# Where operands start in the partition: weight tiles, activations and gap tiles at chosen bytes modulo 128

## The chip, the cores and the metric

One core of one Trainium2 chip runs the kernel as a single program. TensorE (PE in the profile) multiplies, VectorE (DVE), ScalarE (ACT) and GpSimd (POOL) do the elementwise work, SyncE (SP) issues most DMAs. The metric is device time in microseconds of one execution; the median of the runs counts.

## What is computed

A decoder trunk of two layers on x of 256 positions and 1,024 features, in float32. Each layer is a mixer between two half-step SwiGLU FFNs; the first mixer is a chunked gating layer, the second stick-breaking attention whose keys and values come from x ahead of the layer. Cut to what matters:

```python
def swiglu(h, w_in, w_out):                     # w_in 1024 x 5632, w_out 2816 x 1024
    gate, up = jnp.split(h @ w_in, 2, axis=-1)
    return (jax.nn.silu(gate) * up) @ w_out

def chunked_sgu(h, w_in, ln_g, ln_b, w_s, b_s, w_out):
    u, v = jnp.split(jax.nn.gelu(h @ w_in), 2, axis=-1)     # 2048 each
    v = layer_norm(v, ln_g, ln_b)
    ...  # v mixed along positions in chunks of 128 by causal w_s, plus b_s
    return (u * v) @ w_out

def reference(x, ...):
    for i in range(2):
        if i == 1:
            k_shared, v_shared = ...            # rms_norm(x, kv_norm) @ w_kv
        x = x + 0.5 * swiglu(rms_norm(x, ffn_norm[i, 0]), ffn_w_in[i, 0], ffn_w_out[i, 0])
        h = rms_norm(x, mix_norm[i])
        if i == 0:
            x = x + chunked_sgu(h, ...)
        else:
            x = x + stick_breaking_attention(h @ b_w_q[0], k_shared, v_shared) @ b_w_o[0]
        x = x + 0.5 * swiglu(rms_norm(x, ffn_norm[i, 1]), ffn_w_in[i, 1], ffn_w_out[i, 1])
    return rms_norm(x, final_norm)
```

## The kernel before

Activations are kept with features on the 128 partitions: `xT` is x, `xnh` and `xnl` are its normalised high and low parts. Every product is made of three float32r matmuls on such parts (`mm3`): high by low, low by high, high by high, at lines 148 to 150. `split` (line 152) makes the parts of an activation: a ScalarE copy rounds to the high part, a VectorE subtraction leaves the low part.

Weights come as units of 128 x 1,024 float32 (512 KB), in the fixed order in which they are used; `W.add` notes the source of each while the stages are planned. `Weights.run_to` issues their loads on SyncE into seven `raw` buffers and splits each into `whi` (ScalarE, line 81) and `wlo` (VectorE, line 83), nine buffers of each; `Weights.get` runs both some units ahead of their use. There are two kinds:
- First matrices (`cols`): 512 rows by 256 columns of a weight that multiplies x. In gate and up (`ga`, `ua` for the first FFN, then b, c, d), u (`uu`), q and k (`kT`) the weight is the stationary operand and x (`xnh`, `xnl`; `xkh`, `xkl` for k) the moving one, 256 columns. In v (`v`) x is stationary and the weight moves.
- Second matrices (`rows`): 128 rows by 1,024 columns of an output weight. In the FFNs a to c and in the gating layer (`ya`, `yb`, `yc`, `ys`) the weight is stationary and the hidden values `hh`, `hl` of pool `hp` move, 256 columns; in attention's output (`yo` from `oTh`, `oTl`) likewise. In the last FFN (`yo` from `hhd`, `hld`) `hh` and `hl` are stationary and the weight moves, 512 columns.

An FFN runs in eleven steps: 96 matmuls of gate and up for 256 hidden features, and 48 of the output projection two steps behind. While TensorE works on one unit, the loads and splits of later ones go on beside it. Each matmul loads its own stationary operand; TensorE takes all in program order.

Where a tile lies in its partition follows from the order in which the pools are opened (lines 125 to 132, then `sgu`, `att` and `fin`, which take turns in the same space), from the sizes of their tiles, rounded up to 32 bytes, and from what stands ahead: 16,384 bytes of scratch for descriptors and four constants of 32 bytes each. Added up, the places modulo 128 are:

| operand | tiles | bytes modulo 128 |
|---|---|---|
| x | `xT`, `xnh`, `xnl` | 32 |
| loaded weights | `raw` | 96 |
| parts of first and second matrices | `whi`, `wlo` | 96 |
| hidden values, q, attention weights | `hh`, `hl`, `qh`, `ql`, `a0`, `a1` in `hp` | 96 |
| keys, values of attention | `kzh`, `kzl`, `vdh`, `vdl` | 0 |
| x for k and v, attention's output | `xkh`, `xkl`, `oTh`, `oTl` | 0 |
| identity, ones | `ident`, `ones` | 96 |

All slices of these that a matmul reads start at multiples of 512 bytes from the tile's start, so they have the same remainder.

Of the kernel before, what the change touches and what calls it, by code (L numbers as in the profile page):

```python
# [8 lines left out]
F32 = mybir.dt.float32  # L9
F32R = mybir.dt.float32r  # L10
# [5 lines left out]
P = 128  # L16
T = 256
# [5 lines left out]
UNIT = 1024  # L23
# [15 lines left out]
class Weights:  # L39
# [3 lines left out]
    def __init__(self, tc, raw_pool, hi_pool, lo_pool):  # L43
        self.nc = tc.nc
        self.keep_order = tc.keep_in_program_order
        self.strict = False
        self.behind = 0
        self.piece = UNIT
        self.pools = raw_pool, hi_pool, lo_pool
        self.sources = []  # L50
        self.raw = {}
        self.parts = {}
        self.loaded = 0
        self.split = 0

    def add(self, source):
        self.sources.append(source)
        return len(self.sources) - 1

    def order(self, ins):  # L60
# [3 lines left out]
    def run_to(self, load, split):  # L64
        nc = self.nc
        while self.loaded < min(load, len(self.sources)):
            i = self.loaded
            raw = self.pools[0].tile([P, UNIT], F32, tag="raw", name=f"raw{i}")
            src = self.sources[i]
            view = raw if len(src.shape) == 2 else raw.rearrange("p (k c) -> p k c", k=src.shape[1])  # L70
            nc.sync.dma_start(view, src)
            self.raw[i] = raw
            self.loaded += 1
        while self.split < min(split, len(self.sources)):
            i = self.split
            raw = self.raw.pop(i)
            hi = self.pools[1].tile([P, UNIT], F32R, tag="whi", name=f"whi{i}")
            lo = self.pools[2].tile([P, UNIT], F32R, tag="wlo", name=f"wlo{i}")
            for c in range(0, UNIT, self.piece):
                cc = slice(c, c + self.piece)  # L80
                ins = nc.scalar.copy(hi[:, cc], raw[:, cc])  # L81
                self.order(ins)
                ins = nc.vector.tensor_sub(lo[:, cc], raw[:, cc], hi[:, cc].bitcast(F32))  # L83
                self.order(ins)
                if self.behind:
                    self.keep_order(ins)
                    self.behind -= 1
            self.parts[i] = hi, lo
            self.split += 1
# [10 lines left out]
def trunk(  # L100
# [20 lines left out]
    nc = tc.nc  # L121
    x = x[0]
    out = out[0]

    const = ctx.enter_context(tc.tile_pool(name="const", bufs=1))
    act = ctx.enter_context(tc.tile_pool(name="act", bufs=1))
    rawp = ctx.enter_context(tc.tile_pool(name="rawp", bufs=7))
    hip = ctx.enter_context(tc.tile_pool(name="hip", bufs=9))
    lop = ctx.enter_context(tc.tile_pool(name="lop", bufs=9))
    hp = ctx.enter_context(tc.tile_pool(name="hp", bufs=4))  # L130
    scr = ctx.enter_context(tc.tile_pool(name="scr", bufs=8))
    small = ctx.enter_context(tc.tile_pool(name="small", bufs=3))
# [12 lines left out]
    def mm3(o, a, b, first, last):  # L145

        (ah, al), (bh, bl) = a, b
        nc.tensor.matmul(o, al, bh, start=first, stop=False, skip_group_check=True)  # L148
        nc.tensor.matmul(o, ah, bl, start=False, stop=False, skip_group_check=True)  # L149
        nc.tensor.matmul(o, ah, bh, start=False, stop=last, skip_group_check=True)  # L150
# [15 lines left out]
    W = Weights(tc, rawp, hip, lop)  # L166

    def cols(w, c0, kh):
        return w[kh * 512 : (kh + 1) * 512, c0 : c0 + 256].rearrange("(k p) c -> p k c", p=P)

    def rows(w, r0):
        return w[r0 : r0 + P, :]

    def plan_in_out(n, ins, w_out):


        steps = {}
        for j in range(n + 1):
            if j < n:
                steps["in", j] = [[W.add(cols(w, c0 + 256 * j, kh)) for w, c0 in ins] for kh in range(2)]  # L180
            if j:
                steps["out", j - 1] = [W.add(rows(w_out, 256 * (j - 1) + P * m)) for m in range(2)]
        return steps

    def plan_ffn(i, s):
        return plan_in_out(NPAIR, [(ffn_w_in[i, s], 0), (ffn_w_in[i, s], DFF)], ffn_w_out[i, s])
# [3 lines left out]
    plan_u = {}  # L190
    for step in U_STEPS:
        kind, j = step
        if kind == "in":
            plan_u[step] = [W.add(cols(a_w_in[0], 256 * j, kh)) for kh in range(2)]
        elif kind == "out":
            plan_u[step] = [W.add(rows(a_w_out[0], 256 * j + P * m)) for m in range(2)]
    plan01 = plan_ffn(0, 1)
    plan_kv = [[W.add(cols(w_kv, 256 * j, kh)) for kh in range(2)] for j in range(2)]
    plan10 = plan_ffn(1, 0)
    plan_q = [[W.add(cols(b_w_q[0], 256 * j, kh)) for kh in range(2)] for j in range(4)]  # L200
    plan_o = [W.add(rows(b_w_o[0], P * b)) for b in range(8)]
    plan11 = plan_ffn(1, 1)


# [59 lines left out]
    acc = act.tile([P, T], F32, name="acc")  # L264
    rT = act.tile([P, 2], F32, name="rT")

    spare = act.tile([P, P + 1 + 2 * (T + 1)], F32, name="spare")
    rb = spare[:, :T]
    diag = spare[:, T : 2 * T].rearrange("p (n t) -> p n t", n=2)

# [18 lines left out]
            nc.scalar.activation(s, xT[:, d, :], AF.Square)  # L289
            nc.gpsimd.tensor_add(acc, acc, s)  # L290

    eps = const.tile([P, 1], F32, name="eps")
    nc.vector.memset(eps, RMS_EPS)

    def newton(o, root, v, w):
# [79 lines left out]
    class Residual:  # L375
# [8 lines left out]
        def add(self, w, h, first, last, ds=range(KC)):  # L384
            for d in ds:
                mm3(
                    self.at(d), tuple(t[:, d * P : (d + 1) * P] for t in w), h, first and d % 2 == 0, last
                )
# [234 lines left out]
    for kind, j in U_STEPS:  # L623
# [4 lines left out]
        else:  # L628
            h = hs.pop(j)
            for m in range(2):  # L630
                w = W.get(plan_u["out", j][m], UNIT)
# [7 lines left out]

    att = ExitStack()  # L640
    at = att.enter_context(tc.tile_pool(name="att", bufs=1))
    kz = [at.tile([P, 4, 2, T], F32R, name=f"kz{p}") for p in "hl"]
    vd = [at.tile([P, 2, 4, 2, 64], F32R, name=f"vd{p}") for p in "hl"]
    xkh = at.tile([P, KC, T], F32R, tag="bigh", name="xkh")
    xkl = at.tile([P, KC, T], F32R, tag="bigl", name="xkl")
    for t in kz:
# [265 lines left out]
```

## Time and profile before

| | before |
|---|---|
| median of 3 runs | 1003.92 us (1003.63 to 1004.09) |
| profiled execution | 1004.4 us |
| its span, first to last instruction | 1002.7 us |
| PE busy | 982.3 us (98%), 8042 matmul records |
| DVE, ACT, POOL busy | 645.2 us, 504.1 us, 86.5 us |
| DMA | 179.56 MB, 179 GB/s on average |

The profile is of one execution. Matmuls are pipelined: one starts long before the one ahead of it has ended, so a recorded duration of 276 ns doesn't mean that the next one starts 276 ns later. How close they follow is read from the start times in the timeline.

### The profile page before, as it was taken

To read this page: it belongs to the slowest core of one execution; us is meant where nothing else is said; L and a number is where in the kernel's file an instruction comes from. 1 tells how busy PE (TensorE), PEld (TensorE's weight loads), DVE (VectorE), ACT (ScalarE), POOL (GpSimd) and SP (SyncE) were. 2 spreads that over 40 slices of the span, in tenths; PEclk is the share of its full clock that TensorE was granted. 3 is DMA by queue.
4 is the path that set the end of the run, shared out by engine and by line. 5 is a ranking of instruction groups with operands and counts; after the bars stand their busy time and mean duration, and the time that the engine had idled before them with its cause. 6 is when DMAs were issued, how large, how long until landed. Compare 5 with 4: busy or idle time off the path is not lost.

```text
span 1002.7 us, 19306 instructions
## 1 busy us (share of the span) xinstructions
PE 982.3 (98%) x8042; PEld 963.5 (96%) x8042; DVE 645.2 (64%) x823; ACT 504.1 (50%) x690; POOL 86.5 (9%) x126
## 2 busy tenths in 40 slices
PE   8999999999999999999999999999997899999996
PEld 8999999999999999999999999999997899999996
DVE  6864675675866775656569755555678775565644
ACT  6643434475544564444448444444487674444433
POOL 4000000020000300000003000000046320000002
PEclk9999999999999999999999999999999999999999
DMA  9966565647555455666564866665643346656511
GB/s 304 322 195 190 169 189 188 190 143 222 184 177 175 133 191 188 193 188 193 186 195 146 247 189 191 189 193 186 190 149 92 97 147 191 207 172 203 176 42 43
DMA packets 135208, 179.56 MB, mean 179 GB/s; under 512 B 5624, under 2 KB 119376, under 8 KB 135120
## 3 DMA queue, kind: packets, MB, share of 16 engines
q1 hardware_dynamic: 134768, 177.76, 56.7%
q8 instruction: 63, 1.03, 0.4%
q0 software_dynamic: 192, 0.52, 0.2%
q14 instruction: 25, 0.20, 0.1%
q10 hardware_dynamic: 160, 0.05, 0.0%
HBM read 176.73 MB, written 1.05 MB: 177 GB/s over the span
## 4 chain that ended last, share of the span: by engine, by line
PE 89%; DVE 5%; ACT 2%; issue 1%; DMA 1%; POOL 1%; SPq 0%; ACTq 0%; POOLq 0%; DVEq 0%
PE yo L148 2%; PE yo L150 2%; PE yo L149 2%; PE yb L148 2%; PE yb L150 2%; PE yb L149 2%; PE ud L148 2%; PE ud L150 2%; PE gd L148 2%; PE ud L149 2%; PE gb L148 2%; PE gd L150 2%; PE gd L149 2%; PE ub L148 2%; PE gc L150 2%; PE gb L150 2%
## 5 line engine op out<-in xcount | busy, mean ns | idle before, releaser
L81 ACT CAST whi<-raw 128x1024 fp32r<-128x1024 f32 (+1 forms) x333 | 342.7, 1045 | 391.0 <-issue 205.3
L83 DVE TENSOR_TENSOR wlo<-raw,whi 128x1024 fp32r<-128x1024 f32 (+1 forms) x333 | 402.1, 1225 | 200.9 <-ACT whi L81 200.0
L290 POOL TENSOR_TENSOR acc<-acc,sq 128x256 f32<-128x256 f32 x39 | 33.8, 867 | 387.5 <-ACT sq L289 385.6
L148 PE MATMUL ga<-xnh,wlo 128*128 128x256 f32 x176 | 50.1, 285 | 0.0
L148 PE MATMUL ya<-hha,wlo 128*128 128x256 f32 x176 | 49.9, 284 | 0.2 <-DVE xT L399 0.2
L148 PE MATMUL yc<-hhc,wlo 128*128 128x256 f32 x176 | 49.9, 284 | 0.1
L148 PE MATMUL yb<-hhb,wlo 128*128 128x256 f32 x176 | 49.9, 284 | 0.0
L149 PE MATMUL ga<-xnl,whi 128*128 128x256 f32 x176 | 49.3, 280 | 0.5 <-DVE xnl L277 0.5
L149 PE MATMUL ya<-hla,whi 128*128 128x256 f32 x176 | 49.7, 282 | 0.0
L148 PE MATMUL gd<-xnh,wlo 128*128 128x256 f32 x176 | 49.7, 282 | 0.0
L149 PE MATMUL yb<-hlb,whi 128*128 128x256 f32 x176 | 49.7, 282 | 0.0
L149 PE MATMUL yc<-hlc,whi 128*128 128x256 f32 x176 | 49.7, 282 | 0.0
L150 PE MATMUL yb<-hhb,whi 128*128 128x256 f32 x176 | 49.6, 283 | 0.0
L148 PE MATMUL ua<-xnh,wlo 128*128 128x256 f32 x176 | 49.1, 279 | 0.5 <-DVE wlo L83 0.5
L150 PE MATMUL ya<-hha,whi 128*128 128x256 f32 x176 | 49.4, 283 | 0.0
L150 PE MATMUL gd<-xnh,whi 128*128 128x256 f32 x176 | 49.4, 281 | 0.0
L150 PE MATMUL ud<-xnh,whi 128*128 128x256 f32 x176 | 49.4, 281 | 0.0
L148 PE MATMUL ud<-xnh,wlo 128*128 128x256 f32 x176 | 49.4, 281 | 0.0
L149 PE MATMUL ud<-xnl,whi 128*128 128x256 f32 x176 | 49.4, 281 | 0.0
L149 PE MATMUL gd<-xnl,whi 128*128 128x256 f32 x176 | 49.4, 281 | 0.0
L150 PE MATMUL yc<-hhc,whi 128*128 128x256 f32 x176 | 49.4, 283 | 0.0
L150 PE MATMUL ga<-xnh,whi 128*128 128x256 f32 x176 | 49.1, 279 | 0.0
(289 smaller groups left out, 3353.6 us busy)
## 6 DMA issues: line engine op xcount, KB each, us to landing
raw<-in_ffn_w_in_dram SPq DMA_DIRECT2D x176, 512.0 KB, 4.5
raw<-in_ffn_w_out_dram SPq DMA_DIRECT2D x88, 512.0 KB, 4.3
raw<-in_a_w_in_dram SPq DMA_DIRECT2D x32, 512.0 KB, 4.4
raw<-in_a_w_out_dram SPq DMA_DIRECT2D x16, 512.0 KB, 3.3
raw<-in_b_w_q_dram SPq DMA_DIRECT2D x8, 512.0 KB, 4.5
raw<-in_b_w_o_dram SPq DMA_DIRECT2D x8, 512.0 KB, 4.0
raw<-in_w_kv_dram SPq DMA_DIRECT2D x4, 512.0 KB, 4.0
xin<-in_x_dram SPq DMA_DIRECT2D x4, 256.0 KB, 4.9
```

What stands on the lines that cost most here:

```text
L81: ins = nc.scalar.copy(hi[:, cc], raw[:, cc])
L83: ins = nc.vector.tensor_sub(lo[:, cc], raw[:, cc], hi[:, cc].bitcast(F32))
L148: nc.tensor.matmul(o, al, bh, start=first, stop=False, skip_group_check=True)
L149: nc.tensor.matmul(o, ah, bl, start=False, stop=False, skip_group_check=True)
L150: nc.tensor.matmul(o, ah, bh, start=False, stop=last, skip_group_check=True)
L290: nc.gpsimd.tensor_add(acc, acc, s)
```

## The change

Only places change; no instruction is added or taken away. `W.add` takes a place, in elements, and the tiles of `whi` and `wlo` become 32 elements wider, of which 1,024 from that place on are used: 0 for first matrices, 16 (64 bytes) for second ones. Gap tiles of 32, 128, 32 and 64 bytes are put between pools or tiles, `eps` is padded to 128 bytes and `spare` to 2,688, and the descriptor scratch shrinks to 8,192 bytes, which makes room. Added up in the same way, x comes to 0 modulo 128, `raw` to 64, the parts of first matrices to 64 and those of second ones to 0, `hp` to 64, the keys and values stay at 0, `xkh`, `xkl`, `oTh` and `oTl` come to 64, `ident` and `ones` stay at 96.

```diff
-    def add(self, source):
+    def add(self, source, place=0):
         self.sources.append(source)
+        self.places.append(place)
         return len(self.sources) - 1
...
-            hi = self.pools[1].tile([P, UNIT], F32R, tag="whi", name=f"whi{i}")
-            lo = self.pools[2].tile([P, UNIT], F32R, tag="wlo", name=f"wlo{i}")
+            hi, lo = (
+                pool.tile([P, UNIT + 32], F32R, tag=f"w{p}", name=f"w{p}{i}")[:, self.places[i] : self.places[i] + UNIT]
+                for pool, p in zip(self.pools[1:], ("hi", "lo"))
+            )
...
+    def gap(name, size):
+        pool = ctx.enter_context(tc.tile_pool(name=name, bufs=1))
+        pool.tile([P, size // 4], F32, name=f"{name}t")
...
+    gap("gapw", 32)
     rawp = ctx.enter_context(tc.tile_pool(name="rawp", bufs=7))
     hip = ctx.enter_context(tc.tile_pool(name="hip", bufs=9))
     lop = ctx.enter_context(tc.tile_pool(name="lop", bufs=9))
+    gap("gaph", 128)
     hp = ctx.enter_context(tc.tile_pool(name="hp", bufs=4))
...
-                steps["out", j - 1] = [W.add(rows(w_out, 256 * (j - 1) + P * m)) for m in range(2)]
+                steps["out", j - 1] = [W.add(rows(w_out, 256 * (j - 1) + P * m), 16) for m in range(2)]
...
-            plan_u[step] = [W.add(rows(a_w_out[0], 256 * j + P * m)) for m in range(2)]
+            plan_u[step] = [W.add(rows(a_w_out[0], 256 * j + P * m), 16) for m in range(2)]
...
-    plan_o = [W.add(rows(b_w_o[0], P * b)) for b in range(8)]
+    plan_o = [W.add(rows(b_w_o[0], P * b), 16) for b in range(8)]
...
-    spare = act.tile([P, P + 1 + 2 * (T + 1)], F32, name="spare")
+    spare = act.tile([P, P + 1 + 2 * (T + 1)], F32, name="spare", padded_shape=[P, 672])
...
-    eps = const.tile([P, 1], F32, name="eps")
+    eps = const.tile([P, 1], F32, name="eps", padded_shape=[P, 32])
...
+    at.tile([P, 8], F32, name="gapk")
     kz = [at.tile([P, 4, 2, T], F32R, name=f"kz{p}") for p in "hl"]
     vd = [at.tile([P, 2, 4, 2, 64], F32R, name=f"vd{p}") for p in "hl"]
+    at.tile([P, 16], F32, name="gapx")
     xkh = at.tile([P, KC, T], F32R, tag="bigh", name="xkh")
...
-    nc = _bacc.Bacc("TRN2", target_bir_lowering=False, num_devices=1)
+    nc = _bacc.Bacc("TRN2", target_bir_lowering=False, num_devices=1, dynamic_dma_scratch_size=8192)
```

## Rows read from the trace of the kernel before

**Rows 1.** The page: span, busy time of TensorE, and its granted clock in 40 slices

```profile
span 1002.7 us, 19306 instructions
PE 982.3 (98%) x8042; PEld 963.5 (96%) x8042; DVE 645.2 (64%) x823; ACT 504.1 (50%) x690; POOL 86.5 (9%) x126
...
PEclk9999999999999999999999999999999999999999
```

**Rows 2.** The page: the chain that ended last, by engine

```profile
PE 89%; DVE 5%; ACT 2%; issue 1%; DMA 1%; POOL 1%; SPq 0%; ACTq 0%; POOLq 0%; DVEq 0%
```

**Rows 3.** Waits of TensorE, the longest: total us, times, longest us

```profile
PE o L149 <- DVE a0l L154: 6.1, 3, 3.5
```

**Rows 4.** Timeline, FFN c gate and up: start us, us, engine, line; 46 starts apart

```profile
590.59 0.28 PE L148 MATMUL gc<-xnh,wlo 128*128 128x256 f32 x1
...
595.80 0.28 PE L149 MATMUL uc<-xnl,whi 128*128 128x256 f32 x1
```

**Rows 5.** Timeline, FFN d gate and up, 46 starts apart

```profile
856.17 0.28 PE L148 MATMUL gd<-xnh,wlo 128*128 128x256 f32 x1
...
861.59 0.28 PE L149 MATMUL ud<-xnl,whi 128*128 128x256 f32 x1
```

**Rows 6.** Timeline, FFN c output projection, 37 starts apart

```profile
567.77 0.28 PE L150 MATMUL yc<-hhc,whi 128*128 128x256 f32 x1
...
572.21 0.28 PE L148 MATMUL yc<-hhc,wlo 128*128 128x256 f32 x1
```

**Rows 7.** Timeline, FFN d output projection, 512 columns, 19 starts apart

```profile
866.97 0.39 PE L149 MATMUL yo<-wlo,hhd 128*128 128x512 f32 x1
...
871.28 0.39 PE L150 MATMUL yo<-whi,hhd 128*128 128x512 f32 x1
```

**Rows 8.** Timeline, attention's output projection, 22 starts apart

```profile
797.07 0.28 PE L149 MATMUL yo<-oTl,whi 128*128 128x256 f32 x1
...
799.66 0.28 PE L150 MATMUL yo<-oTh,whi 128*128 128x256 f32 x1
```

**Rows 9.** Timeline, the transposes of x after FFN d's first steps, merged

```profile
830.78 1.91 PE L819 MATMUL xb<-ident,xT 128*128 128x128 f32 x16
```

**Rows 10.** Groups by line: out<-in, shape, count, busy us, mean ns, idle before

```profile
L149 PE MATMUL yc<-hlc,whi 128*128 128x256 f32 x176 | 49.7, 282 | 0.0
L149 PE MATMUL gd<-xnl,whi 128*128 128x256 f32 x176 | 49.4, 281 | 0.0
L150 PE MATMUL yc<-hhc,whi 128*128 128x256 f32 x176 | 49.4, 283 | 0.0
L149 PE MATMUL ga<-xnl,whi 128*128 128x256 f32 x176 | 49.3, 280 | 0.5 <-DVE xnl L277 0.5
L149 PE MATMUL ua<-xnl,whi 128*128 128x256 f32 x176 | 48.9, 278 | 0.0
L149 PE MATMUL gb<-xnl,whi 128*128 128x256 f32 x176 | 48.8, 277 | 0.0
L149 PE MATMUL gc<-xnl,whi 128*128 128x256 f32 x176 | 48.6, 276 | 0.0
L149 PE MATMUL ys<-hls,whi 128*128 128x256 f32 x128 | 36.2, 283 | 0.0
L149 PE MATMUL v<-wlo,xnh 128*128 128x256 f32 x128 | 35.7, 279 | 0.0
L149 PE MATMUL uu<-xnl,whi 128*128 128x256 f32 x128 | 35.6, 278 | 0.0
L149 PE MATMUL q<-xnl,whi 128*128 128x256 f32 x64 | 17.9, 279 | 0.0
L149 PE MATMUL yo<-oTl,whi 128*128 128x256 f32 x64 | 17.8, 280 | 0.0
```

**Rows 11.** Stretch of 17 us in FFN c: busy us of each engine, clock, DMA share

```profile
567.00:584.00 17.00, 17.00 (x149) 17.00 (x149) 9.93 (x12) 7.52 (x10) 0.00 (x0) 1.00 0.68 202
```

**Rows 12.** The page: what the GpSimd queue moved

```profile
q0 software_dynamic: 192, 0.52, 0.2%
```

More of the change, by code (lines that the diff above doesn't have):

```diff
@@ L50, in __init__ @@
         self.sources = []
+        self.places = []
         self.raw = {}
```

## The prediction

> **What bounds the kernel now.** Start with the page's busy shares. [...] A busy TensorE says little by itself, so read next the chain that ended last: 89% of it is TensorE, 5% VectorE [rows 2]. Then read what TensorE waited for: its largest wait in the whole span is 6.1 us, in three pieces, in attention [rows 3]. So nothing has to be waited for; the time is how many matmuls there are times how far apart they start. The change adds, removes and reorders no instruction. It can act only on that distance between starts, and the question is whether the distance depends on where operands lie.
>
> It does differ between stages for the same shape (128x128 stationary, 256 moving columns). Take the start times in the timeline, first and last of a stretch with no pause:
> - gate and up of FFN c: 46 steps from 590.59 to 595.80 us, 113.3 ns each [rows 4];
> - gate and up of FFN d, same lines, same tiles' places: 46 steps from 856.17 to 861.59, 117.8 ns [rows 5];
> - output projection of FFN c: 37 steps from 567.77 to 572.21, 120.0 ns [rows 6];
> - output projection of FFN d, 512 columns: 19 steps from 866.97 to 871.28, 226.8 ns [rows 7];
> - output projection of attention: 22 steps from 797.07 to 799.66, 117.7 ns [rows 8].
>
> I call 113.3 the short level, 117.8 the long one. The recorded durations are 276, 281 and 283 ns at 113.3, 117.8 and 120.0 [rows 10], always 163 more than the distance between starts. So the mean duration of a group, less 163, is its distance, and the view that groups by line prices every stage.
>
> Now set these against the places, worked out by adding up tile sizes (the table stands above). In the slowest 256-column stage (120.0) the stationary and the moving operand both start at 96 modulo 128: distance 0. In gate and up they start at 96 and 32: distance 64, and the level is short or long, from the same addresses. In attention's output they start at 96 and 0: distance 32, 117.7. The 512-column rows add a clue: 226.8 less 120.0 is 106.8 ns for 256 more columns, both at distance 0. What the stages pay above 106.8 is 6.5 ns (short), 11 (long), 13.2 (distance 0, at 256 columns and at 512 alike). The cost is per matmul, not per column, and about once or twice the 6.7 ns in which 64 bytes of moving operand go by.
>
> **The change part by part.** *Second matrices at 0, what they meet at 64.* Distance 0 becomes 64 in four output projections, distance 32 becomes 64 in attention's. No row shows distance 64 with both operands on multiples of 64, so I take the nearest rows, distance 64 at 32 and 96, and of their two levels the short one, for it is the one that an undisturbed stage holds (gate of FFN c has a mean of 276 over all 176 of a line [rows 10]). The three FFNs a to c have 528 output matmuls each at 282 to 283 ns: 1,584 x 6.5 = 10.3 us. The gating layer: 384 x 7 (283 against 276) = 2.7 us. Attention: 192 x 4 (280) = 0.8 us. Together 13.8 us. The bounds of this part: at the long level for all of them 1,968 x 2 = 4 us are gained instead; at 109.2 (below) 8 us more than 13.8.
>
> *First matrices at 64, x at 0.* The distance stays 64; both operands move by 32 bytes. At the short level everywhere the stages that are now long, or long part of the time, come down. By the means in [rows 10]: gate and up of FFN a (280 and 278) 1,056 x 3 = 3.2 us; FFN b (277, up alike) 1,056 x 1 = 1.1; FFN c (276) nothing; FFN d (281, up alike) 1,056 x 5 = 5.3; v (279) 384 x 3 = 1.2; u (278) 384 x 2 = 0.8; q (279) 192 x 3 = 0.6. Together 12.2 us. A mean is rounded to 1 ns, so over these 5,184 matmuls this sum is good to 2.6 us. Its bounds: if the long level took over everywhere, 5,184 x 4.5 = 23.3 less the 12.2 that are long already, a loss of 11.1 us; at 109.2, 21 us more gain.
>
> *The last FFN's output, 512 columns.* Distance 0 becomes 64. There is no row of 512 columns at another distance that has no pause in it; by [rows 6] against [rows 4] it would be 6.7 ns for each of about 250, 1.7 us. I leave it at nothing and keep 1.7 for the range.
>
> *Shared keys and values.* 96 matmuls go from distance 32 to distance 0, because x for them lies at 64 now as the first matrices do: 96 x 2.3 (120.0 less 117.7) = 0.2 us lost.
>
> *The rest* has no instruction: gap tiles are never written, and a wider tile is read and written over its 1,024 columns. [...] Casts and subtractions of the split write at new places too. Were they slower, two loaded engines would hide it: in a step of 17 us ScalarE has 7.52 us of work and VectorE 9.93 [rows 11]. DMA share is 0.68 there, so a TensorE that is 3% faster doesn't run into it.
>
> Sum: 13.8 + 12.2 - 0.2 = 25.8 us. The profiled span of 1,002.7 becomes 976.9; the execution took 1.7 us more than its span (1,004.4), and the median of runs lies 0.5 below that execution: 976.9 + 1.7 - 0.5 = 978.1 us.
>
> [...] The rows show the same shape at 113.3 and at 120.0 with the clock at its upper level and no wait [rows 1, 4, 6]. [...]
>
> **The rivals.** *A, both on multiples of 64: a lower level than any here.* 1,024 bytes from a start at 32 modulo 64 touch 17 pieces of 64 bytes, from 0 or 64 only 16. If the 6.5 ns of the short level are that seventeenth piece, and the second 6.7 of distance 0 a collision, both go. The floor is then the transposes at the end, 16 in 1.91 us: 16 steps plus 163 ns make 109.2 each [rows 9]. 5,184 + 1,968 + 192 = 7,344 matmuls x 4.1 = 30 us more, and 250 x 8.4 = 2.1 for 512 columns: 946 us. For it: the excesses are one and two times 6.7. Against it: attention's moving operand starts at 0 already and costs 117.7 [rows 8], and those transposes move 128 columns in that time, half the rate.
>
> *B, the two levels stay mixed.* Short and long come from the same addresses [rows 4, 5], so something in the sequence chooses, and moving both by 32 bytes may leave that. Gate, up, v, u and q then stay as they are (12.2 of 5,184: 2.4 ns above short on average), and the 1,968 output matmuls come to the same mean: 13.8 - 1,968 x 2.4 = 9 us gained, 995 us.
>
> *C, the long level everywhere: slower.* FFN d holds the long level through all eleven steps; if the new places always start there, 11.1 us are lost in the first matrices and 4 gained in the second: 1,011 us. It turns where 78% of the matmuls are long: with a long share f, first matrices lose 23.3f - 12.2 and second ones gain 13.2 - 8.9f, equal at f = 0.79.
>
> *D, the sum and not the distance: slower.* 32 + 96 is 0 modulo 128, 96 + 96 is 64, and the levels of [rows 4] and [rows 6] go with that just as well, as they would if one operand were read from its end. After the change both kinds sum to 64: 120.0 for all, 5,184 x (6.7 - 2.4) = 22 us lost, 1,026 us.
>
> *E, nothing:* levels come from something other than places, 1,003.9 us.
>
> **How the numbers follow.** My forecast, the short level throughout, 0.36; A 0.27; B 0.12; E 0.06; C 0.11; D 0.08. Forecast, A and B are faster by over 0.2% (about what a measurement of this kernel can tell from no change): 0.75; E is the same: 0.06; C and D slower: 0.19. The forecast's own range is 974 to 983, by the rounding of the means and the 1.7 us. The range over cases reaches down past A, 946 less the rounding, to 942, and up past E to 1,005; C and D lie outside.
>
> **What would show it.** Right: the same durations throughout, 276 in gate, up, v, u, q and in the output groups, with no stage at 281 or 283; steps of FFN d as long as those of FFN c in start-to-start. A shows as 272. B shows as 276 in one stage and 281 in another, C as 281 in all, D as 283 in gate and up. Wrong altogether: if the waits of TensorE grow, or its granted clock falls, the price is elsewhere than in places. The shared keys and values, at distance 0 now, should be the slowest 256-column rows, near 283: if they aren't, distance is not what counts.

## The result, and the profile after

| | before | after |
|---|---|---|
| median of 3 runs | 1003.92 us | 988.91 us (988.33 to 990.20) |
| profiled execution | 1004.4 us | 990.2 us |
| its span | 1002.7 us | 988.5 us |

The ratio is 0.9853, with a 95% interval of 0.9831 to 0.9876: 15.0 us faster. The forecast was 978.1 us, so the direction is right and 10.8 us of the gain are missing. 988.91 lies inside the range over all cases, 942 to 1,005, but above the forecast's own, 974 to 983.

The page of the kernel after, against [rows 1, 2]: span, busy time, and the chain that ended last.

```profile
span 988.5 us, 19306 instructions
PE 970.1 (98%) x8042; PEld 950.6 (96%) x8042; DVE 642.8 (65%) x823; ACT 503.5 (51%) x690; POOL 85.5 (9%) x126
...
PE 88%; DVE 5%; ACT 2%; issue 1%; DMA 1%; POOL 1%; SPq 0%; ACTq 0%; POOLq 0%; DVEq 0%
```

The instructions and the shape of the chain are the same, and TensorE is 12.2 us less busy. So the change acted where the prediction looked, on how close matmuls follow each other. Now the timeline of the kernel after, at the same instructions as in [rows 4 to 7] (start us, us, engine, line); the number of starts between the two rows of a pair is the same as there: 46, 46, 37, 19.

```profile
581.02 0.28 PE L160 MATMUL gc<-xnh,wlo 128*128 128x256 f32 x1
586.24 0.28 PE L161 MATMUL uc<-xnl,whi 128*128 128x256 f32 x1
...
845.08 0.28 PE L160 MATMUL gd<-xnh,wlo 128*128 128x256 f32 x1
850.29 0.28 PE L161 MATMUL ud<-xnl,whi 128*128 128x256 f32 x1
...
558.52 0.28 PE L162 MATMUL yc<-hhc,whi 128*128 128x256 f32 x1
562.71 0.28 PE L160 MATMUL yc<-hhc,wlo 128*128 128x256 f32 x1
...
855.52 0.39 PE L161 MATMUL yo<-wlo,hhd 128*128 128x512 f32 x1
859.89 0.40 PE L162 MATMUL yo<-whi,hhd 128*128 128x512 f32 x1
```

FFN c's gate and up stay at 113.3 ns, FFN d's come down from 117.8 to 113.3, FFN c's output from 120.0 to 113.3. The 512-column output goes the other way, from 226.8 to 230.

The groups by line after, against [rows 10] (count, busy us, mean ns of one):

```profile
L161 PE MATMUL yc<-hlc,whi 128*128 128x256 f32 x176 | 48.6, 276 | 0.0
L161 PE MATMUL gd<-xnl,whi 128*128 128x256 f32 x176 | 48.7, 277 | 0.0
L161 PE MATMUL gc<-xnl,whi 128*128 128x256 f32 x176 | 48.7, 277 | 0.0
L161 PE MATMUL v<-wlo,xnh 128*128 128x256 f32 x128 | 35.8, 280 | 0.0
```

`yc` and `gd` gained what was forecast, or nearly. `gc` lost 1 ns, and `v`, which was to fall from 279 to 276, rose to 280.

Put together by stage, from the starts of all matmuls of the two traces. "Distance" is the mean time from one start to the next, without the steps over 150 ns (300 ns with 512 columns), in which TensorE waited, ran at a granted clock of 0.50 (as at 744 to 747 us after), or did something else in between; these stand under everything else. Of the last FFN's 282 output matmuls 36 have 256 columns, so its mean lies below 226.

| stage | distance before, ns | after, ns | gain measured, us | forecast, us |
|---|---|---|---|---|
| gate and up, FFN a | 115.1 | 114.0 | 1.2 | 3.2 |
| FFN b | 114.1 | 113.9 | 0.2 | 1.1 |
| FFN c | 113.5 | 114.4 | -1.0 | 0 |
| FFN d | 117.6 | 114.0 | 3.8 | 5.3 |
| v, u, q together | 116.2 | 115.8 | 0.4 | 2.6 |
| output, FFNs a to c | 119.6 | 113.6 | 9.5 | 10.3 |
| output, gating layer | 119.8 | 115.9 | 1.4 | 2.7 |
| output, attention | 117.9 | 114.4 | 0.7 | 0.8 |
| output, FFN d (512 columns) | 214.1 | 217.1 | -0.8 | 0 |
| shared keys and values | 119.1 | 118.7 | 0.1 | -0.2 |
| everything else | | | -1.3 | 0 |
| sum (the spans) | | | 14.2 | 25.8 |

### The profile page after: what moved, and what is told of

Same layout as the page of the kernel before. It is cut to its first block, busy times and chain, and to the rows that moved or that the text cites. A ratio compares the mean times of both kernels' runs of the same rounds, so it can differ in the third digit from the quotient of the medians.

```text
span 988.5 us, 19306 instructions
## 1 busy us (share of the span) xinstructions
PE 970.1 (98%) x8042; PEld 950.6 (96%) x8042; DVE 642.8 (65%) x823; ACT 503.5 (51%) x690; POOL 85.5 (9%) x126
## 4 chain that ended last, share of the span: by engine, by line
PE 88%; DVE 5%; ACT 2%; issue 1%; DMA 1%; POOL 1%; SPq 0%; ACTq 0%; POOLq 0%; DVEq 0%
PE yo L160 2%; PE yo L162 2%; PE yo L161 2%; PE gc L162 2%; PE uc L162 2%; PE gb L160 2%; PE gc L161 2%; PE gc L160 2%; PE uc L161 2%; PE gb L162 2%; PE gb L161 2%; PE ub L162 2%; PE uc L160 2%; PE ub L161 2%; PE ub L160 2%; PE ud L162 2%
## 5 line engine op out<-in xcount | busy, mean ns | idle before, releaser
L160 PE MATMUL gb<-xnh,wlo 128*128 128x256 f32 x176 | 49.0, 278 | 0.0
L160 PE MATMUL gc<-xnh,wlo 128*128 128x256 f32 x176 | 48.9, 278 | 0.0
L162 PE MATMUL gc<-xnh,whi 128*128 128x256 f32 x176 | 48.8, 277 | 0.0
L162 PE MATMUL uc<-xnh,whi 128*128 128x256 f32 x176 | 48.8, 277 | 0.0
L161 PE MATMUL gc<-xnl,whi 128*128 128x256 f32 x176 | 48.7, 277 | 0.0
L162 PE MATMUL gb<-xnh,whi 128*128 128x256 f32 x176 | 48.7, 277 | 0.0
L161 PE MATMUL gb<-xnl,whi 128*128 128x256 f32 x176 | 48.7, 277 | 0.0
L162 PE MATMUL ua<-xnh,whi 128*128 128x256 f32 x176 | 48.7, 277 | 0.0
L161 PE MATMUL uc<-xnl,whi 128*128 128x256 f32 x176 | 48.7, 277 | 0.0
```

## The experiments

The theory at this point was that of the forecast, amended: distance 64 gives 113.3, and something that isn't distance modulo 128 costs the rest. Against it stood three rivals: multiples of 64 as such, the width of the weight tiles, and a level that is inherited from what ran before. The addresses gave the second one its weight. A weight tile of 1,024 + 32 elements is 4,224 bytes long, 16.5 times 256. So neighbouring buffers of `whi` and of `wlo`, which all started alike modulo 256 before, now alternate by 128. Of the 1,408 gate and up matmuls that read `whi` against `xnh`, stationary minus moving place modulo 256 is 192 in 760 and 64 in 648 (added up from the addresses of the tiles). Below, "distance" of places is stationary minus moving modulo 256, and an order such as 192, 64, 64 names the three matmuls of `mm3`.

**Places alone, in streams.** `e1_map` runs nothing but streams of 36 matmuls from two tiles, for each pair of places.

```diff
+    def stream(name, m, w, n, count):
+        bank = ps.tile([P, 512], F32, tag="ps", name=name)
+        for i in range(count):
+            mo = m // 4 + i // 2 % 2 * n
+            wo = w // 4 + (i % 8) * P
+            order(
+                nc.tensor.matmul(
+                    bank[:, :n],
+                    sta[:, wo : wo + P],
+                    mov[:, mo : mo + n],
...
```

> The decoder is left out; the kernel is streams of float32r matmuls alone, 36 each of 256 moving columns for every pair of eight moving and eight stationary places (16 bytes apart modulo 128), three times over in different orders (the third with one short matmul ahead of each stream), and 24 each of 512 columns for four by four places. The output is x. Theory of distance: start to start 113.3 ns (recorded duration 276) or 117.8 (281) where the places differ by 64, 120 (283) where they are equal, between them elsewhere, whatever the places themselves are. Theory of places on multiples of 64: the pairs (0,64) and (64,0) hold 113.3 in all three orders, (32,96) and (96,32) show 117.8 in some. Theory that what runs ahead chooses the level: the same pair shows different durations in the three orders. 512 columns: distance 0 at 226.8 (389), distance 64 at 230 or more as the changed kernel shows it.

Timeline of the streams, TensorE; the first letter after `p` is the moving place (a is 0, e is 64), the next the stationary one. A row is 36 matmuls, so the next row's start, less its own, divided by 36, is the distance.

```profile
35.30 4.40 PE L137 MATMUL pea<-mov,sta 128*128 128x256 f32 x36
39.54 4.48 PE L137 MATMUL pfa<-mov,sta 128*128 128x256 f32 x36
...
154.58 4.26 PE L137 MATMUL pae<-mov,sta 128*128 128x256 f32 x36
158.68 4.45 PE L137 MATMUL pbe<-mov,sta 128*128 128x256 f32 x36
```

Stationary at 64, moving at 0 (`pae`): 4.10 us for 36, 113.9 ns with the change over from the stream before. The pair turned round (`pea`, moving at 64, stationary at 0) took 4.24 / 36 = 117.8, equal places that are multiples of 32 took 120, and others, in the first of the three orders, 116.7 to 123, but for the four with the stationary place 64 ahead and one more (moving at 112, stationary at 0), at 113.3. No pair was below 113.3, and moving at 32 with stationary at 96 (`pcg`: 113.9) did as well as 0 with 64. That ends rival A: there is no level below, and multiples of 64 are worth nothing in these streams. The third theory showed too: moving at 96 and stationary at 32 took 117.8 ns in two of the three orders of the map and 113.3 in the other (`pgc`, `sgc`, `qgc`), from the same addresses.

**One part alone, one part undone.** `e2_second` takes the kernel before and moves the second matrices alone, with the wider tiles that this needs; x, `hp` and the first matrices' remainder modulo 128 stay. `e3_first` is the kernel after without the 64 bytes of the second matrices.

The first, against before (the second matrices of the gating layer and of attention alike, and the smaller scratch):

```diff
-            hi = self.pools[1].tile([P, UNIT], F32R, tag="whi", name=f"whi{i}")
-            lo = self.pools[2].tile([P, UNIT], F32R, tag="wlo", name=f"wlo{i}")
+            hi, lo = (
+                pool.tile([P, UNIT + 32], F32R, tag=f"w{p}", name=f"w{p}{i}")[:, self.places[i] : self.places[i] + UNIT]
+                for pool, p in zip(self.pools[1:], ("hi", "lo"))
+            )
...
-                steps["out", j - 1] = [W.add(rows(w_out, 256 * (j - 1) + P * m)) for m in range(2)]
+                steps["out", j - 1] = [W.add(rows(w_out, 256 * (j - 1) + P * m), 16) for m in range(2)]
```

The second, against after (the other second matrices alike):

```diff
-                steps["out", j - 1] = [W.add(rows(w_out, 256 * (j - 1) + P * m), 16) for m in range(2)]
+                steps["out", j - 1] = [W.add(rows(w_out, 256 * (j - 1) + P * m)) for m in range(2)]
```

> The second matrices alone are moved by 64 bytes: hidden values stay at 96, second matrices come to 32, x stays at 32 and first matrices at 96. If distance alone decides, the output projections of FFN a, b, c and of the gating layer go from 283 to about 277 as after the change, 10 to 12 us of the 15, time 992 to 994 us, with gate and up as before (FFN d at 281). If both must lie on multiples of 64, they go to 281 at most, about 4 us, 1000 us.

> All of the change but the 64 bytes of the second matrices: x at 0, first matrices at 64, hidden values at 64 and second matrices at 64 too. If distance decides, the output projections stay at 283 (120.0 ns), distance 0, and gate and up of FFN d go to 277, some 4 to 5 us in all: 999 us. If multiples of 64 decide, the output projections go to about 277 as well and the time is 989 us.

`e2_second`: 989.94 us, ratio 0.9862 (0.9846 to 0.9879), as fast as the whole change and 2 to 4 us below what was expected. `e3_first`: 999.85 us, 0.9956 (0.9941 to 0.9972). In `e2_second` FFN d's gate and up fell from 117.6 to 113.7 ns, although nothing in it moved their places modulo 128. Only the tile's length is new there. So the move of x and of the first matrices from 32 and 96 to 0 and 64, which the forecast gave 12.2 us, contributes nothing that can be measured; what these stages gained comes from the width of the tiles. In `e3_first` the outputs stay at 118.8; with alternating tiles they lie at distance 0 and 128.

**The 512 columns.** `e4_last512` puts the last FFN's second matrices back to the place 0.

```diff
-    plan11 = plan_ffn(1, 1)
+    plan11 = plan_ffn(1, 1, 0)
```

> The change with one thing taken back: the second matrices of the last FFN alone, the ones with 512 moving columns, lie at 64 as its hidden values do (distance 0). If 512 columns are faster at distance 0, their recorded duration goes from about 393 back to 389 and their start to start from 230.9 to 226.8 ns, 1.0 us in all. If it is the order or the neighbours that slowed them, they stay at 393.

989.78 us in one run, and the 512-column stage stays at 217.3 (217.1 in the kernel after). The expected 226.8 of undisturbed stretches didn't come back (231.1): with alternating buffers the distance is 0 and 128 by turns. The expectation was wrong in counting modulo 128.

**Modulo 256, and an alternating place.** `e5_map` runs streams again, over 512 bytes: all three of `mm3` alike (c), the first of the three moved by 128 (d), or by 256 (e).

```diff
+            wo = w // 4 + i // 3 % 8 * P + cycle[i % 3] // 4
...
+    CYCLES = dict(c=(0, 0, 0), d=(128, 0, 0), e=(256, 0, 0))
```

> The decoder is left out; streams of matmuls alone, the output is x. The moving operand starts at 0 or 32, the stationary one at 0 to 480 bytes in steps of 32, three matmuls to a slice as in the kernel: all three at one place (c), or the first of three 128 bytes on (d) or 256 bytes on (e), as neighbouring weight tiles lie after the change; 36 matmuls of 256 columns per stream, the places run upwards once and downwards once, and 24 of 512 columns. If only the distance modulo 128 counts, places 128 apart give equal durations in each row and c, d and e are alike: 276 at 64 and 192, 283 at 0 and 128. If the period is 256, 64 and 192 differ (276 against 280) and d lies between them. For 512 columns: 389 at 0 only in c, 393 and more in d, if alternating tiles are what slowed the last FFN.

Timeline of `e5_map`; after `pc` or `pd` stands the moving place (a is 0), then the stationary one in steps of 32 (a is 0, c 64, g 192); `rc` is 512 columns, 24 in a row.

```profile
17.99 4.48 PE L132 MATMUL pcaa<-mov,sta 128*128 128x256 f32 x36
22.30 4.42 PE L132 MATMUL pcab<-mov,sta 128*128 128x256 f32 x36
26.57 4.40 PE L132 MATMUL pcac<-mov,sta 128*128 128x256 f32 x36
30.81 4.39 PE L132 MATMUL pcad<-mov,sta 128*128 128x256 f32 x36
...
162.95 4.25 PE L132 MATMUL pdac<-mov,sta 128*128 128x256 f32 x36
167.04 4.41 PE L132 MATMUL pdad<-mov,sta 128*128 128x256 f32 x36
...
179.78 4.45 PE L132 MATMUL pdag<-mov,sta 128*128 128x256 f32 x36
184.06 4.44 PE L132 MATMUL pdah<-mov,sta 128*128 128x256 f32 x36
...
698.60 5.64 PE L132 MATMUL rcaa<-mov,sta 128*128 128x512 f32 x24
704.08 5.75 PE L132 MATMUL rcab<-mov,sta 128*128 128x512 f32 x24
```

Distance 0: (22.30 - 17.99) / 36 = 119.7 ns. Constant 64: 117.8, here, though the same relation held 113.3 in `e1_map`. In the order 192, 64, 64 (`pdac`): 113.6. In the order 64, 192, 192 (`pdag`): 118.9. With 512 columns, distance 0 gives 5.48 / 24 = 228.3 in this row, change over included (226.7 within the stream); 192 gives 229, 0 and 128 by turns 231, the others 232 to 234. With the first of three moved by 256 every stream took what it took unmoved, and moved by 128 it did not (stationary at 64: 4.24 us unmoved and moved by 256, 4.09 moved by 128): in these streams the period is 256 bytes.

**Distance without alternation.** `e6_minus` and `e7_plus` make the tiles 4,352 bytes long, so that all buffers start alike modulo 256; the distance is 192 throughout in the first, 64 in the second (in v, where x is stationary, 64 and 192).

```diff
-                pool.tile([P, UNIT + 32], F32R, tag=f"w{p}", name=f"w{p}{i}")[:, self.places[i] : self.places[i] + UNIT]
+                pool.tile([P, UNIT + 64], F32R, tag=f"w{p}", name=f"w{p}{i}")[:, self.places[i] : self.places[i] + UNIT]
```

`e7_plus` has this too:

```diff
-    gap("gapw", 32)
+    gap("gapw", 160)
-    gap("gaph", 128)
```

> The change with 256 bytes of room per weight tile in place of 128, so that all tiles lie alike modulo 256 and stationary less moving is 192 modulo 256 in gate, up, u, q and in all output projections of 256 columns, in every matmul. If the period is 128, the time stays at 989 us and durations at 276 to 277. If it is 256 and only plus 64 is good, these stages go to 281 throughout, 4.5 ns on some 7000 matmuls: 1015 us. If the alternation of tiles is what releases the long level, stages lock into 276 or 281 as before the change: 985 to 1010 us.

> The same with stationary less moving at 64 modulo 256 in all of them. Period 128: 989 us. Period 256: 276 throughout in gate, up, u, q and the output projections, no stage at 281, 984 to 986 us, and v, which has its operands the other way round (192), at 281. If alternation is what releases the long level: FFN d at 281 as before the change, 995 us or more.

`e6_minus`: 1011.14 us, ratio 1.0069 (1.0052 to 1.0085). Gate and up of the four FFNs and the outputs of FFNs a to c lie at 117.6 to 117.8; v, at a constant 64 there, lies at 113.9 and u at 116.1. This is close to rival C and its time, 1,011 us: the long level nearly everywhere, from places that all satisfy "64 modulo 128". `e7_plus`: 999.73 us, 0.9952 (0.9937 to 0.9967), with the levels of gate and up mixed as before the change, and the outputs of FFNs a to c at 117.3 to 117.7: not the short level that the pure distance would have given. Its groups by line:

```profile
L160 PE MATMUL gd<-xnl,whi 128*128 128x256 f32 x176 | 49.4, 281 | 0.0
L160 PE MATMUL gc<-xnl,whi 128*128 128x256 f32 x176 | 48.6, 276 | 0.0
```

FFN c short, FFN d long, exactly as in [rows 10].

**The order of the alternation.** `e8_lohi` keeps 4,352 bytes and puts low parts at 192 and high parts at 64 in every product of 256 columns, which is the order 192, 64, 64 in `mm3`, except in v: there the weight's low part is read by the second matmul of the three, so the order is 64, 192, 64, and not the one that the expectation names; the last FFN's second matrices lie at distance 0 throughout. `e9_hilo` turns it round: 64, 192, 192.

The first, against `e7_plus`, with a place for each part:

```diff
-    def add(self, source, place=0):
+    def add(self, source, place=(0, 32)):
...
+                pool.tile([P, UNIT + 64], F32R, tag=f"w{p}", name=f"w{p}{i}")[:, at : at + UNIT]
+                for pool, p, at in zip(self.pools[1:], ("hi", "lo"), self.places[i])
...
+    def plan_ffn(i, s, place=(16, 48)):
...
+    plan_v = [[W.add(cols(a_w_in[0], DA + 256 * j, kh), (32, 0)) for kh in range(2)] for j in range(8)]
...
+    plan11 = plan_ffn(1, 1, (0, 0))
```

The second, against the first (the other products alike):

```diff
-    def add(self, source, place=(0, 32)):
+    def add(self, source, place=(32, 0)):
...
-    def plan_ffn(i, s, place=(16, 48)):
+    def plan_ffn(i, s, place=(48, 16)):
```

> Weight tiles with 256 bytes of room; stationary less moving, modulo 256, is 192 for the first of each three matmuls (the low part of the weight) and 64 for the other two, in every product of 256 columns, v included (there the weight moves, and its places are swapped); in the last FFN's output, 512 columns, it is 0 for all three. The streams alone held 276 from the second matmul on with that order, and 389 for 512 columns at 0. Theory that the order of places within three matmuls decides: 276 in all stages, v too (now 280), last FFN 389; against the changed kernel 3 us less in gate and up, 1.5 in v, 1 each in the gating layer's and the last FFN's output: 981 us. Theory that irregular tiles only shake the long level off and the order is nothing: some stages lock at 281, 990 us or more.

> The same with 64 for the first of three and 192 for the other two. In the streams alone this order gave 118.9 ns start to start. If the order decides: 118.9 in gate, up, v, u, q and the output projections, durations of 280 to 286, 5.6 ns on 7300 matmuls more than the run before this one: about 1020 us. If any alternation does: the same time as that run.

`e8_lohi`: 987.28 us, 0.9819 (0.9806 to 0.9833), where 981 was expected. Gate and up lie at 113.6 to 113.9, outputs of a to c at 113.5 to 113.7, the 512 columns at 214.7; v, where the turned places were to do the same, missed and stayed at 117.8. `e9_hilo`: 1007.61 us in one run, where about 1,020 was expected. Its gate and up are at 118.6 to 118.8 in FFNs b to d, as the streams said, but its outputs at 114.0, which they didn't say.

**Does the order make the level, or keep it?** `e11_hold` sends each order after a stream in another one, forward (p) and back (q). Cases a to g set the stationary place, h to k the moving one; there the distance is 256 less the place in the list, so h is the order 64, 192, 64.

```diff
+    SHORT, LONG = (192, 64, 64), (192, 192, 192)
+    CASES = dict(
+        a=(SHORT, (64,)),
+        b=(LONG, (64,)),
+        c=(LONG, (192,) + (64,) * 11),
+        d=(SHORT, (192,)),
+        e=(SHORT, (64, 192, 192)),
+        f=(LONG, (64, 192, 192)),
+        g=(LONG, SHORT),
+    )
+    TURNED = dict(h=(192, 64, 192), i=(192,), j=(64, 192, 64), k=(64,))
...
+            stream("x" + rn + name, 24, pre)
+            stream("m" + rn + name, 60, main)
```

> The decoder is left out; streams alone, the output is x. Each stream of 60 matmuls of 256 columns at one order of places (stationary less moving, modulo 256) runs behind 24 of another order. Theory that the order brings the level and the short one is then kept: 64 throughout holds 276 behind 24 at 192, 64, 64 (case a) and 281 behind 24 at 192 (b), from the same addresses; one matmul in twelve at 192 (c) frees it or not; 192 throughout behind the short one (d) keeps 276 or falls to 281; 64, 192, 192 goes to 118.9 ns behind either (e, f); 192, 64, 64 goes to 276 even behind the long one (g). Theory that places alone decide: a and b alike. With the places changed on the moving side, as in v: 64 throughout (i) 276, the mixed orders (h, j) 281 as in v of the run before.

Timeline of `e11_hold`; `x` streams have 24 matmuls, `m` streams 60.

```profile
58.80 6.96 PE L132 MATMUL mpe<-mov,sta 128*128 128x256 f32 x60
65.60 2.88 PE L132 MATMUL xpf<-mov,sta 128*128 128x256 f32 x24
...
98.78 7.23 PE L132 MATMUL mpj<-mov,sta 128*128 128x256 f32 x60
105.84 7.23 PE L132 MATMUL mpk<-mov,sta 128*128 128x256 f32 x60
112.91 2.99 PE L132 MATMUL xqg<-mov,sta 128*128 128x256 f32 x24
115.74 6.98 PE L132 MATMUL mqg<-mov,sta 128*128 128x256 f32 x60
122.56 2.88 PE L132 MATMUL xqf<-mov,sta 128*128 128x256 f32 x24
...
179.68 6.96 PE L132 MATMUL mqk<-mov,sta 128*128 128x256 f32 x60
186.48 7.23 PE L132 MATMUL mqj<-mov,sta 128*128 128x256 f32 x60
193.54 6.98 PE L132 MATMUL mqi<-mov,sta 128*128 128x256 f32 x60
200.37 7.22 PE L132 MATMUL mqh<-mov,sta 128*128 128x256 f32 x60
```

The expectation of 118.9 for e and f fell: `mpe`, in the order 64, 192, 192, takes 6.80 us for 60, 113.3 ns. So did everything from a to g, for 67 us, constant 192 included, so b, c and f never saw the long level that they were to start from. Then h, which alternates the moving place, put the stream on the long level, and i, j, k and `xqg` stayed there: `mpj` 7.06 / 60 = 117.7, `mpk` 7.07 / 60 = 117.8, `xqg` 2.83 / 24 = 117.9. `mqg`, in the order 192, 64, 64, was back at 113.3 after four matmuls, and all behind it stayed, until `mqj`. `mqk` has the same addresses as `mpk`, and takes 113.3 where that took 117.8. So at distance 64 or 192 either level can be held; the order 192, 64, 64 can bring the short one back. It isn't needed for that: `mqi`, at a constant 64, was back at 113.3 after five matmuls behind the long `mqj` (6.83 / 60 = 113.8 over all), where `mpi`, from the same addresses, stayed long behind `mph`. The last matmul ahead of `mqi` lay at 192, the last ahead of `mpi` at 64.

**The best version.** `e10_best` is `e8_lohi` with v, and the shared values, at a constant distance of 64, which `e6_minus` had shown at 113.9 for v (the line of the shared values is left out).

```diff
-    plan_v = [[W.add(cols(a_w_in[0], DA + 256 * j, kh), (32, 0)) for kh in range(2)] for j in range(8)]
+    plan_v = [[W.add(cols(a_w_in[0], DA + 256 * j, kh), (32, 32)) for kh in range(2)] for j in range(8)]
```

> The run with 192, 64, 64 once more, but v, where the weight moves, has its operands 64 apart in all three matmuls (shared v 0 to 64 likewise). In the run with 192 throughout elsewhere v had exactly that and stood at 113.9 ns, now it is at 117.8. If the alternation has to be on the stationary side: v at 277, 1.5 us less, 985.5 us. If v was fast there for what ran ahead of it: no change, 987 us.

985.60 us (985.30 to 985.96), ratio 0.9807 (0.9793 to 0.9821), the fastest here. v is at 114.0. Its timeline at the 512 columns of [rows 7]:

```profile
851.44 0.39 PE L160 MATMUL yo<-wlo,hhd 128*128 128x512 f32 x1
855.75 0.40 PE L161 MATMUL yo<-whi,hhd 128*128 128x512 f32 x1
```

19 starts in 4.31 us, 226.8: at a constant distance of 0 the old time is back.

## Why the prediction was right, and where it went wrong

**What bounds the kernel: right.** Every step from waits to starts held. The largest wait is 5.0 us in two pieces, against 6.1 [rows 3], and no instruction moved.

**The second matrices: near in size, 2.2 us too high, and in part by luck.** Forecast 13.8 us, measured 9.5 + 1.4 + 0.7 = 11.6. `e3_first` shows that the 64 bytes are needed: without them the outputs stay at 118.8. They are not enough. At a constant 64 (`e7_plus`) and a constant 192 (`e6_minus`) the outputs of FFNs a to c stood at 117.3 to 117.8, the long level, which the prediction had priced at 4 us; the rest came with the alternating buffers, which it didn't count.

**The first matrices: this term failed.** Forecast 12.2 us, measured 1.2 + 0.2 - 1.0 + 3.8 + 0.4 = 4.6, and that by another cause. The step was to "come to the short level everywhere", on the reasoning that short is what an undisturbed stage holds. The bases don't choose the level (`e2_second` leaves x and `hp` alone and is as fast, 989.94 us), and the distance doesn't either (`e7_plus`, at a constant 64: recorded durations of 276 in FFN c and 281 in FFN d). What was before the eyes in [rows 4, 5], two levels from the same addresses, was the finding and not a disturbance of it. Rival B said so, and had the other half of it wrong: the levels don't stay as they are, because the tiles' new length, which the prediction called a matter of "the rest", alternates the buffers.

How a level is lost and held can be seen in the trace of before. Timeline, the first steps of FFN d:

```profile
810.33 0.28 PE L149 MATMUL gd<-xnl,whi 128*128 128x256 f32 x1
...
812.71 0.28 PE L149 MATMUL ud<-xnl,whi 128*128 128x256 f32 x1
...
812.93 0.50 PE L313 MATMUL pstf<-ones,acc 128*128 128x1 f32 x4
...
813.61 0.28 PE L150 MATMUL gd<-xnh,whi 128*128 128x256 f32 x1
...
818.91 0.28 PE L150 MATMUL ud<-xnh,whi 128*128 128x256 f32 x1
```

The 21 starts up to 812.71 take 2.38 us, 113.3 each. Then four matmuls of one column pass, the norm's statistics, and the 45 starts from 813.61 on take 5.30 us: 117.8. From there FFN d stayed long through all its gate and up steps to the end: the rows of the forecast at 856 us [rows 5] are what was left by an event at 812.9. In `e10_best` the same four matmuls pass at 798.71, at the short level likewise, and the stream comes back:

```profile
798.71 0.50 PE L324 MATMUL pstf<-ones,acc 128*128 128x1 f32 x4
...
799.63 0.28 PE L160 MATMUL gd<-xnl,whi 128*128 128x256 f32 x1
...
800.99 0.28 PE L160 MATMUL gd<-xnl,whi 128*128 128x256 f32 x1
```

Steps of 115, 120 and 119 ns, and then 12 starts in 1.36 us, 113.3. The kernel after lies between the two, because its buffers take turns without regard to which is low and which high. Its FFN c, at the start of a step, and FFN d, in the second half of one (timeline):

```profile
563.05 0.28 PE L160 MATMUL gc<-xnh,wlo 128*128 128x256 f32 x1
...
568.75 0.28 PE L160 MATMUL gc<-xnh,wlo 128*128 128x256 f32 x1
...
574.20 0.28 PE L160 MATMUL yc<-hhc,wlo 128*128 128x256 f32 x1
...
849.15 0.28 PE L160 MATMUL gd<-xnh,wlo 128*128 128x256 f32 x1
...
854.60 0.40 PE L160 MATMUL yo<-whi,hld 128*128 128x512 f32 x1
```

The first 48 matmuls go in the order 64, 192, 192 and take 5.70 us, 118.8 each; the next 48 begin in the order 192, 64, 64 and take 113.5. With six units in a step and nine buffers the pattern repeats every third step: three such steps in FFN c. They are some 0.7 us (3 x 48 x 5 ns) of the 1.0 that FFN c lost, having held the short level throughout before the change, from addresses at which FFN d held the long one. The order alone doesn't do it either: by the addresses, the 48 matmuls of FFN d from 849.15 us on are all in the order 64, 192, 192 too, and take 5.45 us, 113.5 each. Those of FFN c come right behind the output projection, those of FFN d right behind other gate and up matmuls; what ran ahead was at 113.3 in both. Nine such halves of a step, in FFNs a, b and d, ran at the short level.

v, 1.2 us of the term, is the same error from the other side. There the weight moves, so the alternating buffers alternate the moving place, and that kept the long level (117.5), as it did in the streams (`mpj`: 117.7). At a constant 64 v ran at 114.0 (`e10_best`). Whether it is the moving side that does this is not shown: in v, in `mph` and in `mpj` the odd one of the three is the second, and no run alternates the stationary place in that order.

**The 512 columns: the wrong sign.** Left at nothing, with 1.7 us of gain kept for the range; it lost 0.8. What it did best at is a constant distance of 0 modulo 256, which it had (226.7 within the stream in `e5_map`, 226.8 in `e10_best`). The prediction took the 106.8 ns between 120.0 and 226.8 to show a cost "per matmul, not per column", but the 512-column rows of `e5_map` order otherwise: 64 gives 233 and 192 gives 229, where both are below distance 0 at 256 columns.

**Shared keys and values.** They were to go from 117.7 to 120.0 ns (283 recorded), as the test of distance. They are still the slowest 256-column stage, but went from 119.1 to 118.7. They lie at distance 0 and 128 by turns now, and `e5_map` has 119.1 for the order 128, 0, 0 and 118.4 for 0, 128, 128. Before, keys lay at 96 and values at 160, which the prediction read as distance 32 alike; `e5_map` has 117.3 and 120.0 for these. The test was right to fail: in `e5_map` distance counts modulo 256.

**Everything else: 1.3 us lost.** From the first `z` of attention to the first `gd` it is 66.1 us before and 66.7 after, although its output projection became 0.7 us shorter. The stretches of 738 to 743, 743 to 748 and 766 to 772 us after (length, busy times of the engines, granted clock, DMA share, GB/s):

```profile
738.00:743.00 5.00, 2.23 (x14) 1.66 (x12) 3.72 (x5) 3.09 (x8) 3.91 (x8) 1.00 0.71 207
743.00:748.00 5.00, 4.02 (x19) 3.78 (x20) 4.17 (x7) 2.52 (x7) 2.80 (x6) 0.66 0.02 6
766.00:772.00 6.00, 5.01 (x26) 4.82 (x27) 5.13 (x8) 3.28 (x7) 3.30 (x7) 0.72 0.34 118
```

The granted clock was 0.50 for a part of each of the last two (0.50 throughout from 744 to 747 and from 768 to 770 us), for some 3.4 us: the means lack 5 x 0.34 and 6 x 0.28 us of full speed, 1.7 each, which is half of 3.4. In the five microseconds ahead of the first, TensorE was busy for 2.23. The profiled execution of before had none of this: its granted clock was 1.00 from 740 to 810 us. It isn't the change's doing: of the runs of the kernel before beside `e2_second`, those at a mean clock of 0.999 took 1003.1 to 1003.3 us and those at 0.995 or 0.996 took 1003.9 to 1005.1, and the kernel after took 988.33 at 0.999, 988.91 and 990.20 at 0.995.

**Rivals.** A fell with `e1_map`: nothing below 113.3. D fell: places that sum to 64 run at 113.3 (FFN c's output in the kernel after). C came near at other places: `e6_minus`, 1011.14 against its 1,011. E fell too: with the same instructions and only places changed, the time went from 1003.92 us to 988.91. What in the hardware makes places count, no run shows.

**The sum.** 25.8 us forecast, 14.2 measured in the spans: 7.6 us short in the first matrices, 2.2 in the second, 0.8 in the 512 columns, 1.3 in everything else, less 0.3 in keys and values, 11.6 together. By the medians it is 10.8, because the profiled execution after lies 1.3 us above its median and the one before 0.5.

Taken one at a time, alternation without the right distance for the outputs (`e3_first`) is worth 4.3 us, and distance without alternation 4.9 at a constant 64 (`e7_plus`) and a loss of 6.5 at a constant 192 (`e6_minus`). Together they are worth 15.

## What to carry to other kernels

Where a profile shows the same matmul at two speeds from the same addresses, as here at 113.3 and 117.8 ns, ask what holds each and what switches them before you price a move of the addresses. Look at places over at least twice the period that seems to explain the rows (here 128 bytes seemed to, and `e5_map` showed 256), and count the lengths of rotating buffers among the places: a change of padding that only "makes room" can move every second buffer, as the tiles of 4,224 bytes did here, by 128. In this kernel, low parts of the weights at 192 and high parts at 64 gave 113.5 to 113.9 ns in the FFNs (`e8_lohi`); the reverse gave up to 118.8 in gate and up (`e9_hilo`), a constant 192 gave 117.8 (`e6_minus`), and equal places 120.0 (FFN c's output before, [rows 6]).

## What the runs showed that was not expected

- For 128x128 by 128x256 float32r with a load for each matmul, the distance from the moving to the stationary place counted modulo 256 bytes in `e5_map`: 119.7 ns at 0, 118.6 at 128, 117.8 at 64 and at 192. `e11_hold` held 113.3 at 64 (`mpa`) and at 192 (`mpd`).
- At 64 and 192 either level was held. The same addresses ran at 113.3 and at 117.8 for 60 matmuls and more (`mqk`, `mpk`), and across four matmuls of one column the distance went from 113.3 to 117.8 (812.93 us before).
- The order 192, 64, 64, with the stationary place alternating, brought the short level back within four matmuls (`mqg`: 113.7 over all 60), and a constant 64 did so once within five (`mqi`: 113.8 over all 60). The orders 64, 192, 64 and 192, 64, 192, with the moving place alternating, gave the long one (`mph`: 117.8; `mpj`: 117.7).
- With 512 columns the best in `e5_map` was distance 0 (226.7 within the stream); most others took 233.
- Places alone moved this kernel between 1011.14 us (`e6_minus`) and 985.60 (`e10_best`).

Two things stay open. The order 64, 192, 192 held 113.3 in `e11_hold`, and in `e9_hilo` ran at 118.6 in gate and up but at 114.0 in the outputs; what ran just before differs, and in the kernel after the same order ran at 118.8 behind an output projection and at 113.3 behind gate and up. What it is in the matmuls ahead that decides, no run separates. And which of the two levels a stream takes after an interruption wasn't settled: only that it mostly keeps it.
